# Linear attention: the value and gate projections of a head as one product of 512 columns

## The chip, the cores and the metric

The kernel runs on one core of a Trainium2 chip. The metric is device time in microseconds. Five engines work side by side, each through its own queue in order: TensorE (PE in the rows, its weight loads PEld), VectorE (DVE), ScalarE (ACT), GpSimdE (POOL), and SyncE (SP), which here only issues DMAs. An engine whose next instruction waits does nothing else until that wait is over.

## The reference

Two layers of a hybrid encoder, 512 tokens of width 1024. Each layer normalises, projects, runs three mixers (a state-space mixer, gated linear attention "GLA", and neighbourhood attention), gates and sums them, and ends in an MLP. The change concerns GLA's projections:

```python
h = _rms(x) * norm_mix_w[l]
u = h @ w_in[l]
(z, xbc, dt_f, dt_b, gq, gk, gv, gg, ga_f, ga_b, nq, nk, nv, gate_logits) = jnp.split(u, splits, axis=-1)
...
v = gv.reshape(Bsz, S, GLA_HEADS, GLA_DV)      # 4 heads, 256 value columns each
...
o = gla_chunked(q, k, v, g_f) + _rev(gla_chunked(_rev(q), _rev(k), _rev(v), _rev(g_b)))
o = _rms(o) * gla_norm_w[l] * jax.nn.silu(gg).reshape(Bsz, S, GLA_HEADS, GLA_DV)
```

Of a head, `gv` (values) and `gg` (the output gate, through SiLU) are each 512 tokens by 256 columns.

## The kernel before

Every large product is computed three times over in parts, high weights by high input, high by low, low by high, to keep float32 accuracy on the float32r path. Weights come in **granules** of 128 x 1024 numbers (512 KB) in an order fixed by the list `ks`. `wprep` issues the DMA of a granule into a raw tile `wr` (SP queue), ScalarE copies it to the high part `wh` (L285), VectorE subtracts to get the low part `wl` (L287). `wr`, `wh` and `wl` have three buffers each, used in turn, and `wget` keeps three granules in preparation.

`feat` makes a product with features down the partitions: 8 steps of 3 matmuls of 512 columns (L304 to L306), 24 in all, one granule. `token` makes one with tokens down the partitions, as GLA needs for values and gates: for each of four blocks of 128 tokens, 8 steps of 3 matmuls of 256 columns (L321 to L323). One call serves the values of a head, a second one the gate, with two granules each: 96 matmuls a call, 192 a head, 1536 in the kernel (4 heads, 2 layers). Results land in PSUM tiles `pt` of 128 x 512, two token blocks in one. These and the `pf` tiles of `feat` share a pool `mm` of **two** buffers, used in turn: each new `pt` or `pf` has to wait until the one before the last has been read out. ScalarE reads `pt` out into `G_gvg` (L643), four reads of 128 x 256 a call: plain copies for the values, SiLU for the gate.

`gla_proj(h)` runs the two `token` calls, then `feat` for q and k. `gla_mix(h)` follows: from the small product `G_ga` come, for each of two directions `d`, Abs, Exp and Ln on ScalarE (L670, L673, L674), a subtraction on GpSimdE (L676), a scan on VectorE (L682), and three more Exp on ScalarE (L685, L686, L692). Its matrix part needs q and k. ScalarE has to load a table (ACT_TABLE_LOAD) when it goes from one of SiLU, Exp or Ln to another.

The order of the calls is: projection 0, mix 0, first branch product (16 `feat`), projection 1, mix 1, projection 2, mix 2, projection 3, mix 3. The instructions of each engine are then put into an order by a scheduler ahead of time; `hp()` marks weight preparation and PSUM reads as urgent. Once built, the order on an engine is fixed.

Of the kernel before, what the change touches and what calls it, by code (L numbers as in the profile page):

```python
# [9 lines left out]
F32R = mybir.dt.float32r  # L10
I32 = mybir.dt.int32
AF = mybir.ActivationFunctionType
# [58 lines left out]
def host_arrays(w):  # L71

    w = {k: np.asarray(v) for k, v in w.items()}
    f = np.float32

    def feat(m):
        return m.reshape(KT, P, P).transpose(1, 0, 2).reshape(P, D)

    pk = np.empty((L, NG, P, D), f)
    for l in range(L):  # L80
        wi = w["w_in"][l]
        br = (w["w_branch_na"][l], w["w_branch_gla"][l], w["w_branch_ssd"][l])
        gorder = (2, 1, 0)
        for k, i in KIDX.items():
            o = pk[l, i]
            n = k[0]
            if n in ("nk", "nq", "nv", "gq", "gk", "xs", "B", "C", "z"):
                base = {"nk": O_NK, "nq": O_NQ, "nv": O_NV, "gq": O_GQ, "gk": O_GK, "xs": O_XBC,
                        "B": O_XBC + 1024, "C": O_XBC + 1280, "z": O_Z}[n]
                o[:] = feat(wi[:, base + P * k[1]: base + P * (k[1] + 1)])  # L90
            elif n == "sm":
                ga = wi[:, O_GA: O_GA + 32]
                o[:] = feat(np.concatenate([ga, ga, ga, wi[:, O_DT: O_DT + 32]], axis=1))
            elif n == "gvg":
                h, q = k[1], k[2]
                c = (O_GV, O_GG)[q // 2] + 256 * h
                m = wi[NT * (q % 2): NT * (q % 2 + 1), c: c + 256]
                o[:] = m.reshape(4, P, 256).transpose(1, 0, 2).reshape(P, D)
            elif n == "gate":
                c = O_GATE + D * gorder[k[1]] + P * k[2]  # L100
                o[:] = feat(wi[:, c: c + P])
            elif n == "br":
                o[:] = feat(br[k[1]][:, P * k[2]: P * (k[2] + 1)])
            elif n == "wo":
                o[:] = feat(w["w_out"][l][:, P * k[1]: P * (k[1] + 1)])
            elif n == "f1":
                o[:] = feat(w["w_ff1"][l][:, P * k[1]: P * (k[1] + 1)])
            elif n == "f2":
                q, j = k[1], k[2]
                o[:] = feat(w["w_ff2"][l][D * q: D * (q + 1), P * j: P * (j + 1)])  # L110

    col = np.zeros((L, P, NCOL), f)
    a2 = np.zeros((L, P, 2, NT), f)
    for l in range(L):
        c = col[l]
        c[:, C_NMIX: C_NMIX + 8] = w["norm_mix_w"][l].reshape(8, P).T
        c[:, C_NMLP: C_NMLP + 8] = w["norm_mlp_w"][l].reshape(8, P).T
        c[:, C_CW: C_CW + 60] = w["ssd_conv_w"][l].reshape(5, 12, P).transpose(2, 1, 0).reshape(P, 60)
        c[:, C_CB: C_CB + 12] = w["ssd_conv_b"][l].reshape(12, P).T
        c[:, C_SSDN: C_SSDN + 8] = w["ssd_norm_w"][l].reshape(8, P).T  # L120
        c[:, C_GLAN: C_GLAN + 2] = w["gla_norm_w"][l].reshape(2, P).T
        c[:, C_WQ] = np.concatenate([w["na_q_norm_w"][l]] * 2)
        c[:, C_WK] = np.concatenate([w["na_k_norm_w"][l]] * 2)
        c[:, C_GBF: C_GBF + 4] = w["gla_a2_bias_f"][l].reshape(4, P).T
        c[:, C_GBB: C_GBB + 4] = w["gla_a2_bias_b"][l].reshape(4, P).T
        c[:, C_D: C_D + 8] = np.repeat(w["ssd_d"][l].reshape(8, 2).T, 64, axis=0)
        c[:, C_ALOG: C_ALOG + 32] = np.concatenate([w["ssd_a_log_f"][l], w["ssd_a_log_b"][l]])[None]
        c[:, C_DTB: C_DTB + 32] = np.concatenate([w["ssd_dt_bias_f"][l], w["ssd_dt_bias_b"][l]])[None]
        for r in range(3):
            a2[l, 32 * r: 32 * r + 16, 0] = w["gla_a2_f"][l]  # L130
            a2[l, 32 * r + 16: 32 * r + 32, 1] = w["gla_a2_b"][l]


    con = np.zeros((P, NCON), f)
    con[:, K_ID: K_ID + P] = np.eye(P)
    con[:, K_TF: K_TF + P] = np.triu(np.ones((P, P)))
    con[:, K_TB: K_TB + P] = np.tril(np.ones((P, P)))
    con[:, K_ONE: K_ONE + P] = 1.0
    con[:, K_RST: K_RST + NT] = (np.arange(NT) % 64 != 0)[None]
    for t in range(8):  # L140
        con[:64, K_BS + 32 * t + 2 * t] = 1.0
        con[64:, K_BS + 32 * t + 2 * t + 1] = 1.0
    for r in range(32):
        h = r % 16
        con[r, K_OH + r] = 1.0
        con[32 + r, K_OH + r] = 1.0
        if r < 16:
            con[r, K_E + 64 * h: K_E + 64 * (h + 1)] = 1.0
            con[32 + r, K_E + 64 * h: K_E + 64 * (h + 1)] = 1.0


    bias = np.empty((L, 8, 3, P, 2, 256), f)
    pos = np.arange(NT)
    row, colm = (pos // 8) % 8, (pos // 64) * 8 + pos % 8
    for v, cb in enumerate((0, 1, 3)):
        q = np.arange(P) + P * cb
        k = np.arange(256) + NA_START[cb]
        ro = row[k][None, :] - row[q][:, None] + 7
        d = colm[k][None, :] - colm[q][:, None]
        ws = np.clip(colm[q] - 8, 0, 64 - 16)  # L160
        rel = colm[k][None, :] - ws[:, None]
        ok = (rel >= 0) & (rel < 16)
        co = np.clip(d, -15, 15) + 15
        b = np.where(ok[None, None], w["na_rpb"][:, :, ro, co], f(NEG))
        bias[:, :, v] = b.reshape(L, 8, 2, P, 256).transpose(0, 1, 3, 2, 4)

    xt = np.ascontiguousarray(w["x"].reshape(NT, KT, P).transpose(1, 2, 0))
    return {"xt": xt, "pk": pk, "col": col, "a2": a2, "con": con, "bias": bias}
# [31 lines left out]
def trunk(tc, a, out, layers=L, dbg=None):  # L200
    nc = tc.nc
    V, S, G, T = nc.vector, nc.scalar, nc.gpsimd, nc.tensor
    with ExitStack() as ctx:
# [72 lines left out]

        order, pend = [], []

        def wprep(l, key):
            raw = pw.tile([P, D], F32, tag="wr", bufs=3, name=nm("wr"))  # L280
            nc.sync.dma_start(raw, a["pk"][l, KIDX[key]])
            hi = pw.tile([P, D], F32R, tag="wh", bufs=3, name=nm("wh"))
            lo = pw.tile([P, D], F32R, tag="wl", bufs=3, name=nm("wl"))
            with hp():
                S.activation(hi, raw, AF.Copy)  # L285
            with hp():
                V.tensor_tensor(lo, raw, f(hi), ALU.subtract)  # L287
            pend.append((l, key, hi, lo))

        def wget(l, key):  # L290
            while len(pend) < 3 and order:
                wprep(*order.pop(0))
            l_, k_, hi, lo = pend.pop(0)
            assert (l_, k_) == (l, key), (k_, key)
            return hi, lo
# [10 lines left out]
                T.matmul(ps, lhsT=lo[:, c], rhs=rh[k], start=False, stop=k == KT - 1)  # L306
            return ps

        def token(l, keys, rh, rl):

            w = [wget(l, key) for key in keys]
            ps = []
            for b in range(4):
                if b % 2 == 0:
                    ps.append(psm("pt"))
                o = ps[-1][:, 256 * (b % 2): 256 * (b % 2) + 256]
                s = slice(P * b, P * (b + 1))
                for k in range(KT):
                    hi, lo = w[k // 4]
                    c = slice(256 * (k % 4), 256 * (k % 4) + 256)  # L320
                    T.matmul(o, lhsT=rh[k][:, s], rhs=hi[:, c], start=k == 0, stop=False)  # L321
                    T.matmul(o, lhsT=rh[k][:, s], rhs=lo[:, c], start=False, stop=False)  # L322
                    T.matmul(o, lhsT=rl[k][:, s], rhs=hi[:, c], start=False, stop=k == KT - 1)  # L323
            return ps

        def lnexp(after):

# [54 lines left out]
        for l in range(layers):  # L382
# [225 lines left out]
            def branch(b, j, bh, bl, g_=None):  # L608
# [9 lines left out]
                if b:  # L618
# [2 lines left out]

            px_ = Phase(tc, f"X{l}", {"xs": 4, "bc": 2}, {})
            ph = Phase(tc, f"G{l}", {"A": 1, "kwT": 2, "st0": (3, 256), "st1": (3, 256), "t1": 3, "t2": 3, "w": 2,
                                     "gvg": 8, "bs": 2, "gst": 1, "q": 1, "k": 1, "a2": (2, 256), "kx": (2, 256)},
                       {"ga": 1, "at": 1, "x": 2, "po": 2})
            ps = feat(l, ("sm", 0), xh, xl)
            with hp():
# [5 lines left out]
            glh, gll = [], []  # L633

            def gla_proj(h):
                v_, g_ = [], []
                for n, (r_, fn) in enumerate(((v_, AF.Copy), (g_, AF.Silu))):
                    ps = token(l, [("gvg", h, 2 * n), ("gvg", h, 2 * n + 1)], xh, xl)
                    for i in range(2):
                        t_ = ph.t("gvg", (P, 2, 256))  # L640
                        for b in (0, 1):
                            with hp():
                                S.activation(t_[:, b], ps[i][:, 256 * b: 256 * b + 256], fn,  # L643
                                             scale=rtok[:, 2 * i + b: 2 * i + b + 1])
                        r_.append(t_)
                ps = feat(l, ("gq", h), xh, xl)
                q_ = ph.t("q")
                with hp():
# [437 lines left out]
```

## Time and profile before

| what | value |
|---|---|
| median of 3 runs | 2444.17 us (2443.42 to 2446.34) |
| the profiled execution's own time | 2445.34 us |
| its span in the trace | 2443.6 us |
| TensorE busy | 2428.9 us, 99% of the span |
| ScalarE busy | 1157.9 us, 47% |
| VectorE busy | 1435.6 us, 59% |
| granted TensorE clock | 1.0 |

The time of a run and its span differ by 1.7 us, what lies around the span. Layer 0's GLA runs from about 214 to 545 us, layer 1's from about 1427 to 1760 us; neighbourhood attention goes ahead of it, the state-space mixer follows. In the rows, `x48` is a count, a duration in us stands behind a start, and the bracket says how long the engine had been idle and what it waited for.

### The profile page before, as it was taken

The numbers are of one execution on the slowest core, as the hardware profiler recorded it, in microseconds if no ns is written. First come the engines' busy times: TensorE is split into PE (matmuls) and PEld (weight loads), VectorE is DVE, ScalarE is ACT, GpSimd is POOL, SyncE is SP. The second block draws the span as 40 slices with busy tenths as digits, with TensorE's granted clock in tenths as the row PEclk, the third lists the DMA queues.
The fourth block names the chain that finished last, engine by engine and source line by source line (L and its number), as shares of the span: only waits on it lengthen the run. The fifth ranks groups of instructions, "written<-read, shape, count | busy, mean of one in ns | idle before, by whom it ended". The sixth has DMA issues, their size and how long they took to land.

```text
span 2443.6 us, 32635 instructions
## 1 busy us (share of the span) xinstructions
PE 2428.9 (99%) x12656; PEld 2063.0 (84%) x12656; DVE 1435.6 (59%) x2156; ACT 1157.9 (47%) x2055; POOL 393.3 (16%) x333
## 2 busy tenths in 40 slices
PE   9999999999999999999999999999999999999999
PEld 7899889987888888888888998899888888888887
DVE  6786534587976553443457755345989665534443
ACT  4475425556855342332335754265578543422321
POOL 3132101112431210000122321011134212100000
PEclk9999999999999999999999999999999999999999
DMA  5231222224533323223333222222245332232222
GB/s 183 89 105 63 90 87 79 72 77 134 166 112 126 100 96 97 95 95 100 124 125 97 86 69 88 87 73 85 78 139 168 102 129 95 95 100 98 93 97 87
DMA packets 84603, 249.38 MB, mean 102 GB/s; under 512 B 9824, under 2 KB 15840, under 8 KB 84448
## 3 DMA queue, kind: packets, MB, share of 16 engines
q1 hardware_dynamic: 84016, 246.85, 30.8%
q8 instruction: 100, 1.64, 0.3%
q10 hardware_dynamic: 432, 0.45, 0.1%
q14 instruction: 55, 0.45, 0.1%
HBM read 242.80 MB, written 4.46 MB: 101 GB/s over the span
## 4 chain that ended last, share of the span: by engine, by line
PE 96%; DMA 1%; DVE 1%; ACT 1%; issue 0%; SPq 0%; DVEq 0%
PE pf L305 14%; PE pf L304 14%; PE pf L306 14%; PE F_pf L304 11%; PE F_pf L306 11%; PE F_pf L305 11%; PE pt L322 3%; PE pt L323 3%; PE pt L321 3%; PE N_po L580 2%; PE N_pt L570 1%; PE S_x L956 1%; PE S_py L945 1%; PE N_sc L554 1%; PE N_sc L555 1%; PE G_x L743 1%
## 5 line engine op out<-in xcount | busy, mean ns | idle before, releaser
L285 ACT ACTIVATE wh<-wr 128x1024 fp32r<-128x1024 f32 x378 | 400.3, 1059 | 926.4 <-PE F_pf L305 429.7
L287 DVE TENSOR_TENSOR wl<-wr,wh 128x1024 fp32r<-128x1024 f32 x378 | 486.8, 1288 | 179.0 <-ACT wh L285 177.0
L304 PE MATMUL pf<-xh,wh 128*128 128x512 f32 x1232 | 485.6, 395 | 6.7 <-DVE gl L603 3.8
L305 PE MATMUL pf<-xl,wh 128*128 128x512 f32 x1232 | 486.3, 395 | 0.2 <-DVE xl L349 0.2
L306 PE MATMUL pf<-xh,wl 128*128 128x512 f32 x1232 | 485.1, 394 | 0.0
L304 PEld LDWEIGHTS pf<-xh,wh 128*128 128x128 f32 x1232 | 232.2, 189 | 57.1 <-DVE gl L603 4.6
L306 PEld LDWEIGHTS pf<-xh,wl 128*128 128x128 f32 x1232 | 232.1, 188 | 49.2 <-issue 1.5
L305 PEld LDWEIGHTS pf<-xl,wh 128*128 128x128 f32 x1232 | 232.1, 188 | 47.9 <-DVE xl L349 0.9
L304 PE MATMUL F_pf<-Ah,wh 128*128 128x512 f32 x640 | 248.3, 389 | 0.0
L305 PE MATMUL F_pf<-Al,wh 128*128 128x512 f32 x640 | 247.7, 389 | 0.0
L306 PE MATMUL F_pf<-Ah,wl 128*128 128x512 f32 x640 | 247.7, 389 | 0.0
L306 PE MATMUL F_pf<-xh,wl 128*128 128x512 f32 x512 | 200.0, 391 | 0.0
L305 PE MATMUL F_pf<-xl,wh 128*128 128x512 f32 x512 | 199.2, 389 | 0.0
L304 PE MATMUL F_pf<-xh,wh 128*128 128x512 f32 x512 | 199.2, 389 | 0.0
L1063 DVE TENSOR_TENSOR F_x<-F_x,F_pf 128x512 f32<-128x512 f32 x64 | 44.0, 687 | 206.7 <-PE F_pf L306 206.7
L322 PE MATMUL pt<-wl,xh 128*128 128x256 f32 x512 | 146.2, 286 | 0.0
L321 PE MATMUL pt<-wh,xh 128*128 128x256 f32 x512 | 145.4, 285 | 0.0
L323 PE MATMUL pt<-wh,xl 128*128 128x256 f32 x512 | 144.9, 284 | 0.0
L306 PEld LDWEIGHTS F_pf<-Ah,wl 128*128 128x128 f32 x640 | 120.1, 188 | 25.0
L305 PEld LDWEIGHTS F_pf<-Al,wh 128*128 128x128 f32 x640 | 120.2, 188 | 24.9
L304 PEld LDWEIGHTS F_pf<-Ah,wh 128*128 128x128 f32 x640 | 120.1, 188 | 24.9
L1056 DVE SCALAR_TENSOR_TENSOR F_v<-F_pf,rx 128x512 f32<-128x512 f32 x64 | 44.1, 691 | 159.6 <-PE F_pf L306 159.5
(315 smaller groups left out, 4243.0 us busy)
## 6 DMA issues: line engine op xcount, KB each, us to landing
wr<-pk SPq DMA_DIRECT2D x378, 512.0 KB, 3.3
N_bias<-bias SPq DMA_DIRECT2D x48, 256.0 KB, 2.8
S_E<-acd SPq DMA_DIRECT2D x32, 256.0 KB, 4.4
S_eB<-acd SPq DMA_DIRECT2D x32, 256.0 KB, 3.7
S_eb<-ead SPq DMA_DIRECT2D x64, 96.0 KB, 3.6
F_x<-xt SPq DMA_DIRECT2D x15, 256.0 KB, 5.4
xd<-F_x SPq DMA_DIRECT2D x8, 256.0 KB, 2.0
F_x<-xd SPq DMA_DIRECT2D x8, 256.0 KB, 5.5
```

The source lines that it names most:

```text
L285: S.activation(hi, raw, AF.Copy)
L287: V.tensor_tensor(lo, raw, f(hi), ALU.subtract)
L304: T.matmul(ps, lhsT=hi[:, c], rhs=rh[k], start=k == 0, stop=False)
L305: T.matmul(ps, lhsT=hi[:, c], rhs=rl[k], start=False, stop=False)
L306: T.matmul(ps, lhsT=lo[:, c], rhs=rh[k], start=False, stop=k == KT - 1)
L321: T.matmul(o, lhsT=rh[k][:, s], rhs=hi[:, c], start=k == 0, stop=False)
L322: T.matmul(o, lhsT=rh[k][:, s], rhs=lo[:, c], start=False, stop=False)
L323: T.matmul(o, lhsT=rl[k][:, s], rhs=hi[:, c], start=False, stop=k == KT - 1)
L554: T.matmul(sc[:, i], lhsT=q_[hh][:, qs], rhs=kh[hh][:, kr], start=True, stop=False)
L580: T.matmul(po[:, P * cb: P * (cb + 1)], lhsT=z_[:, c: c + P], rhs=pts[hh][:, i, kb], start=hh + kb == 0, stop=hh + kb == 2)
L1056: V.scalar_tensor_tensor(v_, ps, 0.0, rbc, ALU.max, ALU.mult)
L1063: V.tensor_tensor(xT[j], xT[j], ps, ALU.add)
```

## The change

`token` is called once a head, with four granules. A granule now holds 256 input rows of values and gate side by side, so that a matmul has 512 columns (256 of values, 256 of gate) and a token block fills a whole `pt` tile. That makes 96 matmuls of 512 columns a head in place of 192 of 256. All four granules have to be at hand together; the fourth gets a buffer of its own in the GLA phase (`own`, tiles `G_wh`, `G_wl`), and the next two granules are asked for when the first two have been used for the last time. The order is written out: token blocks 0 and 1 through all granules, then 2 and 3. `done` reads a block out: one copy, one SiLU.

```diff
-        def wprep(l, key):
+        def wprep(l, key, own=None):
             raw = pw.tile([P, D], F32, tag="wr", bufs=3, name=nm("wr"))
             nc.sync.dma_start(raw, a["pk"][l, KIDX[key]])
-            hi = pw.tile([P, D], F32R, tag="wh", bufs=3, name=nm("wh"))
-            lo = pw.tile([P, D], F32R, tag="wl", bufs=3, name=nm("wl"))
+            if own:
+                hi, lo = own.t("wh", (P, D), F32R), own.t("wl", (P, D), F32R)
+            else:
+                hi = pw.tile([P, D], F32R, tag="wh", bufs=3, name=nm("wh"))
+                lo = pw.tile([P, D], F32R, tag="wl", bufs=3, name=nm("wl"))
...
+        def wfill(n=3):
+            while len(pend) < n and order:
+                wprep(*order.pop(0))
...
+            wfill()
+            wprep(*order.pop(0), own)
+            w = []
...
+            ps = {}
+            for n, (g, b) in enumerate(((0, 0), (0, 1), (1, 0), (1, 1), (2, 0), (3, 0), (2, 1), (3, 1),
+                                        (0, 2), (1, 2), (0, 3), (1, 3), (2, 2), (3, 2), (2, 3), (3, 3))):
+                if g == 0:
+                    ps[b] = psm("pt")
                 s = slice(P * b, P * (b + 1))
...
+                hi, lo = w[g]
+                for k in (2 * g, 2 * g + 1):
+                    c = slice(NT * (k % 2), NT * (k % 2 + 1))
+                    T.matmul(ps[b], lhsT=rh[k][:, s], rhs=hi[:, c], start=k == 0, stop=False)
+                    T.matmul(ps[b], lhsT=rh[k][:, s], rhs=lo[:, c], start=False, stop=False)
+                    T.matmul(ps[b], lhsT=rl[k][:, s], rhs=hi[:, c], start=False, stop=k == KT - 1)
+                if g == 3:
+                    done(b, ps[b])
+                if n == 11:
+                    wfill(2)
...
+                def done(b, ps):
+                    for n, (t_, fn) in enumerate(((v_, AF.Copy), (g_, AF.Silu))):
+                        with hp():
+                            S.activation(t_[b // 2][:, b % 2], ps[:, 256 * n: 256 * n + 256], fn,
+                                         scale=rtok[:, b: b + 1])
+
+                token(l, [("gvg", h, i) for i in range(4)], xh, xl, ph, done)
```

The scheduler's order moves with it, on ScalarE above all. The first place is head 1 of layer 0, on ScalarE, from the read-out of token blocks to the weights of q and k. `wh_37..` and `wh_39..` are the high weights that follow the head's own in the kernel before; `G_t` with `G_ga` and `G_bs` is `gla_mix(1)`. Before:

```order
L692 ACTIVATE G_w_3795<-G_w_3795 128x512 [waits Pool_49]
L285 ACTIVATE wh_3591<-wr_3589 128x1024 [waits DMAHW5_49,PE_49]
L643 ACT_TABLE_LOAD
L643 ACTIVATE G_gvg_3696<-pt_3644,tcol_648 128x256 [waits PE_49]
L643 ACTIVATE G_gvg_3696<-pt_3644,tcol_648 128x256
L285 ACTIVATE wh_3701<-wr_3699 128x1024 [waits DMAHW6_49]
L285 ACTIVATE wh_3734<-wr_3732 128x1024 [waits DMAHW7_49,PE_49]
L285 ACTIVATE wh_3923<-wr_3921 128x1024 [waits DMAHW0_49,DVE_49,PE_49]
L670 ACTIVATE G_t_72_3782<-G_ga_3780,col_120 128x512 [waits PE_49]
L673 ACT_TABLE_LOAD
L673 ACTIVATE G_t_72_3782<-G_t_72_3782 128x512 [waits Activation_49]
L674 ACT_TABLE_LOAD
```

The same place of the changed kernel, where L660 is the read-out, L288 the copy of weights, L688 to L710 the mix (`wh_3471` and `wh_3477` are the weights of q and k, `pt_3443` is token block 2):

```order
L691 ACTIVATE G_t_78_3592<-G_t_78_3592 128x512 [waits Activation_49]
L692 ACT_TABLE_LOAD
L692 ACTIVATE G_t_78_3592<-G_t_78_3592 128x512 [waits Activation_49]
L703 ACT_TABLE_LOAD
L703 ACTIVATE G_t_78_3592<-G_bs_3614 128x512 [waits DVE_49]
L704 ACTIVATE G_t_79_3593<-G_bs_3614 128x512
L710 ACTIVATE G_w_3620<-G_w_3620 128x512 [waits Pool_49]
L288 ACTIVATE wh_3471<-wr_3469 128x1024 [waits DMAHW4_49,PE_49]
L288 ACTIVATE wh_3477<-wr_3475 128x1024 [waits DMAHW5_49,PE_49]
L660 ACTIVATE G_gvg_3374<-pt_3443,tcol_648 128x256 [waits PE_49]
L660 ACT_TABLE_LOAD
L660 ACTIVATE G_gvg_3376<-pt_3443,tcol_648 128x256
```

Before, the second direction's chain of the mix stood behind the read-out of the last block and the weights that come next; now that chain stands ahead of the read-out of block 2 and ahead of the weights of q and k.

The second place is TensorE where the head's token product ends and q begins. Before:

```order
L321 MATMUL pt_3644<-wh_3475,xh_182 128x256
L322 MATMUL pt_3644<-wl_3476,xh_182 128x256
L323 MATMUL pt_3644<-wh_3475,xl_183 128x256
L304 MATMUL pf_3705<-xh_154,wh_3585 128x512 [waits Activation_49]
L305 MATMUL pf_3705<-xl_155,wh_3585 128x512
L306 MATMUL pf_3705<-xh_154,wl_3586 128x512 [waits DVE_49]
```

And now:

```order
L335 MATMUL pt_3456<-G_wh_3385,xh_182 128x512
L336 MATMUL pt_3456<-G_wl_3386,xh_182 128x512
L337 MATMUL pt_3456<-G_wh_3385,xl_183 128x512
L310 MATMUL pf_3515<-xh_154,wh_3471 128x512 [waits PE_49,Activation_49]
L311 MATMUL pf_3515<-xl_155,wh_3471 128x512
L312 MATMUL pf_3515<-xh_154,wl_3472 128x512 [waits DVE_49]
```

In both, q's tile takes the PSUM buffer of the tile before the last: before, `pt_3595`, blocks 0 and 1 of the gate, whose last matmul stands 36 places ahead of q's first; now `pt_3443`, block 2, whose last two matmuls stand only 12 places ahead of q's first.

The third place is head 0 on ScalarE. Before:

```order
L285 ACTIVATE wh_2577<-wr_2575 128x1024 [waits DMAHW2_49]
L643 ACT_TABLE_LOAD
L643 ACTIVATE G_gvg_2685<-pt_2587,tcol_648 128x256 [waits PE_49]
L643 ACTIVATE G_gvg_2685<-pt_2587,tcol_648 128x256
L285 ACTIVATE wh_2583<-wr_2581 128x1024 [waits DMAHW4_49,PE_49]
L643 ACTIVATE G_gvg_2688<-pt_2636,tcol_648 128x256 [waits PE_49]
L643 ACTIVATE G_gvg_2688<-pt_2636,tcol_648 128x256
L285 ACTIVATE wh_2693<-wr_2691 128x1024 [waits DMAHW5_49,DVE_49]
```

And now (`pt_2531` is block 2, `wh_2559` and `wh_2565` the weights of q and k):

```order
L688 ACTIVATE G_t_29_2670<-G_ga_2668,col_120 128x512 [waits PE_49]
L346 ACT_TABLE_LOAD
L691 ACTIVATE G_t_29_2670<-G_t_29_2670 128x512 [waits Activation_49]
L692 ACTIVATE G_t_29_2670<-G_t_29_2670 128x512 [waits Activation_49]
L703 ACTIVATE G_t_29_2670<-G_bs_2687 128x512 [waits DVE_49]
L704 ACTIVATE G_t_30_2671<-G_bs_2687 128x512
L288 ACTIVATE wh_2559<-wr_2557 128x1024 [waits DMAHW2_49,PE_49]
L710 ACTIVATE G_w_2693<-G_w_2693 128x512 [waits DMAHW3_49,Pool_49]
L288 ACTIVATE wh_2565<-wr_2563 128x1024 [waits DMAHW4_49,PE_49]
L660 ACTIVATE G_gvg_2462<-pt_2531,tcol_648 128x256 [waits PE_49]
L660 ACT_TABLE_LOAD
L660 ACTIVATE G_gvg_2464<-pt_2531,tcol_648 128x256
```

Before, nothing of the mix stood among the read-outs of head 0; now the first direction's chain stands between the read-outs of block 1 and block 2.

## Rows read from the trace of the kernel before

**Rows 1.** The page: busy time of each engine, share of the span, instructions.
```profile
PE 2428.9 (99%) x12656; PEld 2063.0 (84%) x12656; DVE 1435.6 (59%) x2156; ACT 1157.9 (47%) x2055; POOL 393.3 (16%) x333
```

**Rows 2.** Busy time by stretch, us: PE, PEld, DVE, ACT, POOL, clock, DMA share, GB/s.
```profile
214.00:372.00 158.00, 158.00 (x908) 139.13 (x907) 72.22 (x113) 65.24 (x110) 17.75 (x16) 1.00 0.24 79
372.00:545.00 173.00, 173.00 (x1082) 156.02 (x1082) 108.39 (x179) 98.81 (x153) 25.11 (x19) 1.00 0.23 74
```

**Rows 3.** What TensorE waited for, whole span: us in total, times, longest.
```profile
PE pf L304 <- DVE gl L603: 3.8, 2, 2.1
```

**Rows 4.** Instructions of the tile pt: duration ns min/median/max.
```profile
L321 PE MATMUL pt<-wh,xh x512: 277/283/467, 217.1 to 1687.8; 128*128 128x256 f32 x171
...
L643 ACT ACTIVATE G_gvg<-pt,tcol x64: 456/468/477, 239.9 to 1688.7; 128x256 f32<-128x256 f32 x64
```

**Rows 5.** Timeline of TensorE, head 1: token product, then q and k.
```profile
376.86 0.40 PE L667 MATMUL G_ga<-G_gst,G_a 96*128 96x512 f32 x1
377.10 0.40 PE L321 MATMUL pt<-wh,xh 128*128 128x256 f32 x2
...
387.18 0.40 PE L304 MATMUL pf<-xh,wh 128*128 128x512 f32 x1
...
398.10 0.40 PE L667 MATMUL G_ga<-G_gst,G_a 96*128 96x512 f32 x1
```

**Rows 6.** Timeline of ScalarE, head 1.
```profile
377.31 0.69 ACT L670 ACTIVATE G_t<-G_ga,col 128x512 f32<-128x512 f32 x1
378.01 1.28 ACT L329 ACT_TABLE_LOAD   x1
379.30 0.63 ACT L673 ACTIVATE G_t<-G_t 128x512 f32<-128x512 f32 x1
...
383.18 0.84 ACT L643 ACTIVATE G_gvg<-pt,tcol 128x256 f32<-128x256 f32 x2 [1.28 <-PE pt L323]
...
385.33 0.63 ACT L685 ACTIVATE G_t<-G_bs 128x512 f32<-128x512 f32 x1
385.87 0.62 ACT L686 ACTIVATE G_t<-G_bs 128x512 f32<-128x512 f32 x1
...
386.91 1.05 ACT L285 ACTIVATE wh<-wr 128x1024 fp32r<-128x1024 f32 x1
```

**Rows 7.** Timeline of ScalarE, GpSimdE and VectorE, head 0: from Ln to the next Exp.
```profile
267.92 0.63 ACT L674 ACTIVATE G_t<-G_t 128x512 f32<-128x512 f32 x1
268.68 1.29 POOL L676 TENSOR_TENSOR G_t<-G_t,G_t 128x512 f32<-128x512 f32 x1 [21.82 <-ACT G_t L674]
270.00 1.22 DVE L682 TENSOR_TENSOR_SCAN G_bs<-con,G_t 128x512 f32<-128x512 f32 x1 [2.72 <-POOL G_t L676]
...
271.26 0.63 ACT L685 ACTIVATE G_t<-G_bs 128x512 f32<-128x512 f32 x1 [0.17 <-DVE G_bs L682]
```

**Rows 8.** Timeline of TensorE, start of projection 1: transposes of the branch.
```profile
363.04 1.03 PE L780 MATMUL G_x<-con,G_gvg 128*128 128x128 f32 x8
```

**Rows 9.** Timelines of ScalarE, TensorE, VectorE at the end of neighbourhood attention.
```profile
236.96 1.08 ACT L572 ACTIVATE N_pT<-N_pt 128x512 f32<-128x512 f32 x2 [4.50 <-PE N_pt L570]
...
239.77 1.05 PE L580 MATMUL N_po<-N_pT,N_vb 128*128 128x128 f32 x8
...
239.99 1.23 DVE L287 TENSOR_TENSOR wl<-wr,wh 128x1024 fp32r<-128x1024 f32 x1 [7.76 <-ACT wh L285]
```

**Rows 10.** Timeline of TensorE: the kernel's start, and its longest later idle time.
```profile
8.38 1.22 PE L304 MATMUL pf<-xh,wh 128*128 128x512 f32 x2 [1.77 <-ACT xh L348]
...
10.41 0.63 PE L306 MATMUL pf<-xh,wl 128*128 128x512 f32 x1
...
14.25 0.75 PE L304 MATMUL pf<-xh,wh 128*128 128x512 f32 x2
...
609.69 0.50 PE L304 MATMUL pf<-xh,wh 128*128 128x512 f32 x1 [2.12 <-DVE gl L603]
610.03 0.39 PE L305 MATMUL pf<-xl,wh 128*128 128x512 f32 x1
```

More of the change, by code (lines that the diff above doesn't have):

```diff
@@ L95, in host_arrays @@
                 h, q = k[1], k[2]
-                c = (O_GV, O_GG)[q // 2] + 256 * h
-                m = wi[NT * (q % 2): NT * (q % 2 + 1), c: c + 256]
-                o[:] = m.reshape(4, P, 256).transpose(1, 0, 2).reshape(P, D)
+                r = slice(256 * q, 256 * (q + 1))
+                m = np.concatenate([wi[r, c + 256 * h: c + 256 * (h + 1)] for c in (O_GV, O_GG)], axis=1)
+                o[:] = m.reshape(2, P, NT).transpose(1, 0, 2).reshape(P, D)
             elif n == "gate":
@@ L288, in wprep @@
             pend.append((l, key, hi, lo))
+        def wfill(n=3):
+            while len(pend) < n and order:
+                wprep(*order.pop(0))
         def wget(l, key):
-            while len(pend) < 3 and order:
-                wprep(*order.pop(0))
+            wfill()
             l_, k_, hi, lo = pend.pop(0)
@@ L307, in feat, with token @@
             return ps
[L309 to L316, printed above, removed]
-                s = slice(P * b, P * (b + 1))
[L318 to L324, printed above, removed]
+        def token(l, keys, rh, rl, own, done):
+            wfill()
+            wprep(*order.pop(0), own)
+            w = []
+            for key in keys:
+                l_, k_, hi, lo = pend.pop(0)
+                assert (l_, k_) == (l, key), (k_, key)
+                w.append((hi, lo))
+            ps = {}
[3 more added lines that the diff above has]
+                    ps[b] = psm("pt")
+                s = slice(P * b, P * (b + 1))
+                hi, lo = w[g]
[8 more added lines that the diff above has]
+                    wfill(2)
         def lnexp(after):
@@ L623, in trunk @@
             ph = Phase(tc, f"G{l}", {"A": 1, "kwT": 2, "st0": (3, 256), "st1": (3, 256), "t1": 3, "t2": 3, "w": 2,
-                                     "gvg": 8, "bs": 2, "gst": 1, "q": 1, "k": 1, "a2": (2, 256), "kx": (2, 256)},
+                                     "gvg": 8, "bs": 2, "gst": 1, "q": 1, "k": 1, "a2": (2, 256), "kx": (2, 256),
+                                     "wh": (1, D), "wl": (1, D)},
                        {"ga": 1, "at": 1, "x": 2, "po": 2})
@@ L635, in gla_proj @@
             def gla_proj(h):
[L636 to L645, printed above, removed]
+                v_ = [ph.t("gvg", (P, 2, 256)) for _ in range(2)]
+                g_ = [ph.t("gvg", (P, 2, 256)) for _ in range(2)]
+                def done(b, ps):
[4 more added lines that the diff above has]
+                token(l, [("gvg", h, i) for i in range(4)], xh, xl, ph, done)
                 ps = feat(l, ("gq", h), xh, xl)
```

## Prediction

> **What bounds the kernel now.** I read the page first: TensorE is busy for 2428.9 us, 99% of a span of 2443.6 us [rows 1]. The reader is to see that only two things can move the time: fewer TensorE microseconds, or new idle time on TensorE. Busy time by stretch says the same of the place of the change: in layer 0's GLA TensorE works without a hole, 158.00 of 158 us and 173.00 of 173 us, at a granted clock of 1.00, while ScalarE works for 65 and 99 us and the DMA engines for about a quarter [rows 2]. The waits of TensorE say how good the cover is: the largest entry of the whole span is 3.8 us, in a normalisation outside GLA [rows 3]. So ScalarE and VectorE have slack on average; what matters is whether one of their results is late at a certain matmul. For that I read the timeline of one head, the part of an average that no busy share shows.
>
> The profiled execution took 2445.34 us, 1.2 us above the median of 2444.17. I make the sum against the former and take the 1.2 off at the end.
>
> **What the wider product removes.** There are 512 matmuls on each of the three lines of `token` (4 heads, 2 layers, 64 a line and head), 1536 together, all 128 x 256. Rows 4 show such a group, a median of 283 ns from issue to end; durations overlap, so the price is the pitch. In head 1, 84 matmuls of 256 columns start between 377.10 and 387.18: 0.120 us each. The 48 of 512 columns that follow take from 387.18 to 398.10: 0.2275 us each [rows 5]. A pair of 256 costs 0.240 and its successor 0.2275, so the change saves 12.5 ns on 768 pairs, **9.6 us**. The successor has the same pattern as the 512-column matmuls of `feat` (two of three share their stationary operand), hence the same pitch.
>
> The Trainium skill ("TensorE: Matmul & The Clock Gate", section "Back-to-back issue gap") gives a single matmul N/2.4 + 2.5 ns at the full clock. By that a pair of 256 costs 218.4 ns, one of 512 215.8, and the change saves 768 x 2.5 ns, 1.9 us in place of 9.6. The trace has a fixed part of about 12.5 ns in a stream of this kernel, and I go by the trace.
>
> **What stays.** ScalarE reads out as many pieces as before, 64 in a group of 0.47 us each [rows 4]; granules, bytes, copies and subtractions are the same, and the order has as many table loads (75) as before. The next granules are asked for when granules 0 and 1 are used up; then 24 matmuls of the head remain, 5.5 us by the pitch above. Copy, subtraction and start cost 1.05 [rows 6] and 1.23 us [rows 9], and the raw data come ahead of that at a quarter of the DMA engines' time [rows 2]. I cost it at nothing. Without that cover each head would pay up to those 2.3 us, 18 us in all; nothing in the order asks for it.
>
> **What the order adds, head 1.** This is the main term. A PSUM tile now holds values and gate of one block, and the two buffers go round by block: block 2 gets block 0's, q's tile gets block 2's. q can start only when ScalarE has read out block 2, copy and SiLU. Before, the tile in question had been done 36 matmuls earlier; now its last two stand 12 matmuls ahead of q. And ScalarE has the whole chain of the second direction of mix 1, then the weights of q and k, ahead of that read-out.
>
> I add up both engines from U, the start of the last matmul of block 0. A reader starts 0.45 us after the start of the last matmul (376.86 to 377.31) [rows 5, 6]. ScalarE then has, in its printed order:
> - copy 0.47, table load 1.28, SiLU 0.47 [rows 4, 6]: until U + 2.7. Table load and three Exp of the first direction, 1.28 + 2 x 0.54 + 0.63 [rows 6]: U + 5.6.
> - Block 1: two reads at a pitch of 0.36 (0.84 for two less 0.47) and a table load: U + 7.8.
> - Abs 0.69, table load 1.28, Exp 0.63, table load 1.28 [rows 6]: the Ln starts at U + 11.65.
> - From Ln over GpSimdE (1.29) and VectorE's scan (1.22) to the next Exp it takes 3.34 us, 267.92 to 271.26 [rows 7]: U + 15.0. Three Exp: U + 16.65. Weights of q and k, 1.05 each: U + 18.7.
> - Read-out of block 2, copy, table load, SiLU, 0.36 + 1.28 + 0.47: U + 20.85, and q starts some 0.1 later, U + 20.95.
>
> TensorE in that time has the small gate product (0.24), 12 matmuls of block 1 and 48 of blocks 2 and 3: 60 x 0.2275 + 0.24 + 0.23 = 14.1 us. It wants q at U + 14.1 and gets it at U + 20.95: a stall of **6.9 us**, in each layer. What waits behind it is all of TensorE, q, k, the whole of mix 1; nothing else is at hand for it, since its order is fixed. Before, the same wait ended long ahead, since the mix stood behind the read-outs.
>
> **Head 0.** Three smaller stalls, worked out in the same way.
> - At the end of neighbourhood attention the head's fourth granule is copied behind two copies `N_pT` of 0.36 to 1.08 us [rows 9], and its subtraction (1.23) follows. TensorE has 8 matmuls of about 1 us to cover it [rows 9]. About 1.0 us is left.
> - Block 0's read-out has a table load between copy and SiLU: 0.45 + 0.47 + 1.28 + 0.47 + 0.1 = 2.8 us. TensorE can cover 1.6 (five matmuls, the small product): 1.2 us.
> - Block 2's read-out stands behind the first direction's chain of mix 0 and the weights of q and k. From T, the start of block 0's last matmul: block 0 read 2.7, block 1 (0.84) 3.5, Abs, table load, Exp (0.69 + 1.28 + 0.63) 6.1, Ln to the next Exp (3.34) 9.5, three Exp and two weights (0.54 + 0.63 + 0.63 + 2 x 1.05) 13.4, read-out (0.36 + 1.28 + 0.47) 15.5, less some 0.2 of overlaps: T + 15.3. TensorE starts block 2 at T + 2.9 and wants q 48 matmuls later, T + 13.95: 1.35 us.
>
> Together 3.6 us a layer. Heads 2 and 3, which run interleaved with the mix before, came out with no wait in the same addition. At the start of projection 1 eight transposes of 1.03 us for the branch stand on TensorE [rows 8], and its 16 `feat` ahead of them; they cover the head's first granules.
>
> **The clock.** At the start of the kernel 9 matmuls take from 10.41 to 14.25 us, 0.427 each, against 0.2275 later [rows 5, 10]: that is the lower of the two levels, 1.2 GHz, and idle time stands ahead of it. An idle time of 2.12 us at 609.69 was followed by a pitch of 0.34 and then 0.23, so the clock held [rows 10]. A wait of 6.9 us is three times that one; the trace has no other of its size. The bounds for what it costs in clock are 0 and 2.9 us a stall (the start ran at half rate from 8.38 to 14.25 us [rows 10], and half of these 5.87 is what it lost). It is nearer to the start's than to 2.12 us, so I take **2.0 us** each, 4.0 in all.
>
> The Trainium skill (the same page, section "HAM oscillation — how this bites in real kernels") also says that a stall of several microseconds between matmuls brings TensorE back at the lower clock; that speaks for the upper part of these bounds, and no row here shows such a stall inside the kernel.
>
> **The sum.** −9.6 + 2 x (6.9 + 3.6) + 4.0 = +15.4 us: 2445.34 + 15.4 − 1.2 = **2459.6 us**.
>
> **The rivals.**
> - *ScalarE's chain is not late* (0.19). ScalarE has 40% slack over the stretch [rows 2]; were its chain ahead of my addition by 7 us, because the first direction's Exp are already done when the block 0 read-out comes and the second direction's Abs needs no wait, all stalls would fall under TensorE's work. Then only the saving stays: 2444.2 − 9.6 = 2434.6, faster. It decides at the read-out of block 2 in head 1: the gain outweighs the loss if the stalls add to less than 4.8 us a layer. Against it: the chain has 14 steps in strict order and 4 table loads, with two engines in between, and each duration has its row.
> - *Only half of it* (0.09). The 6.9 us are lost, but to head 0 nothing, or the chain is about 4 us shorter: −9.6 + 7.2 to 9.6 gives 2441.8 to 2444: no change.
> - *The rule's pitch* (0.05). If a 512-column matmul of `token` costs 2.5 ns less than a pair, since each needs its own weight load, the saving is 1.9 us and the sum +23.1: 2467.3. The rows of `feat` speak against it. The page's gap named above is this case; the trace does not agree with it.
> - *The clock holds, or falls fully.* Inside the forecast: 2455.6 without a loss, 2461.4 with 2.9 us a stall.
>
> **How the numbers follow.** The forecast has 0.67. Its own range is 2449 (stalls a third shorter, no loss of clock: −9.6 + 14) to 2466 (stalls a quarter longer). To hold 8 in 10 the range reaches down over the "half" case: 2441 to 2467; outside is mainly the faster rival. A measurement of this kernel can tell about 0.2%, 4.9 us, from no change, so below 2439.3 is faster: 0.19. Between 2439.3 and 2449.1: 0.09. Above, 0.72.
>
> **What would show it.** In the profile after: a wait of TensorE of about 7 us, twice, ahead of q's first matmul in head 1, ended by ScalarE's read-out `G_gvg` (the SiLU), with ScalarE busy or waiting for the scan all that time; waits of 1.2 to 1.4 us twice in head 0, and none of weight in heads 2 and 3. 512-column matmuls of `pt` at a pitch of 0.2275, and so TensorE busy less by 9.6 us but for the clock; a pitch near 0.43 for some microseconds behind each 7 us wait if the clock falls, 0.23 if not. I would be wrong if q's wait is short, which means that ScalarE is through with mix 1 earlier than I add up, or if a wait for weights (`wl`, VectorE) comes in at another place.

## The result and the profile after

The changed kernel takes 2464.88 us (median of 5 runs, 2463.14 to 2465.78), the kernel before 2445.65 us in the same runs: a ratio of 1.0078, with a 95% interval of 1.0065 to 1.0091. That is 19.2 us slower. The forecast was 2459.6 us, +15.4. The two profiled executions differ by 17.7 us in span (2461.3 against 2443.6), and all that follows is told on these spans.

TensorE's busy time hardly moved (2427.5 us against 2428.9): what the wider products save is taken up by matmuls that run more slowly elsewhere, as the granted clock below shows, and the rest of the loss is idle time. Waits of TensorE, changed kernel, whole span (in us: total, times, longest):

```profile
PE pf L310 <- ACT G_gvg L660: 14.3, 4, 6.4
PE pf L310 <- DVE gl L620: 4.4, 2, 2.3
...
PE pt L335 <- ACT G_gvg L660: 1.9, 2, 0.9
...
PE N_po L597 <- ACT N_pT L589: 0.6, 2, 0.3
PE N_pt L587 <- POOL N_s L583: 0.3, 2, 0.2
```

Two names are new: q (`pf`) and the token product (`pt`) wait for the read-out `G_gvg`, which TensorE never waits for in the kernel before. 14.3 us in 4 times, the longest 6.4: two long waits, one a layer, and two short ones of 0.8. The last two lines are the end of neighbourhood attention.

Where they lie shows in busy time by stretch of layer 0, changed kernel (columns as in [rows 2]): head 0 and the branch; head 1's token product with the wait behind it; its q and k; the rest.

```profile
216.80:366.30 149.50, 147.12 (x731) 123.21 (x730) 67.03 (x105) 64.94 (x108) 14.29 (x15) 1.00 0.25 81
366.30:395.40 29.10, 22.82 (x101) 18.33 (x99) 9.98 (x14) 23.42 (x32) 5.78 (x6) 0.95 0.14 43
395.40:408.20 12.80, 12.72 (x48) 10.41 (x49) 5.39 (x6) 3.71 (x6) 0.00 (x0) 0.85 0.52 165
408.20:564.50 156.30, 156.21 (x767) 130.69 (x765) 103.53 (x180) 77.32 (x127) 17.74 (x13) 1.00 0.22 70
```

The same work in the kernel before, by the same view:

```profile
217.13:363.50 146.37, 146.37 (x823) 128.09 (x822) 66.05 (x104) 62.15 (x106) 16.77 (x15) 1.00 0.25 82
363.50:387.10 23.60, 23.60 (x199) 23.56 (x198) 7.72 (x10) 13.76 (x21) 2.33 (x2) 1.00 0.20 67
387.10:398.30 11.20, 11.20 (x51) 9.28 (x51) 4.98 (x6) 5.22 (x7) 0.00 (x0) 1.00 0.44 140
398.30:556.00 157.70, 157.70 (x959) 140.64 (x957) 108.77 (x186) 87.82 (x139) 22.79 (x17) 1.00 0.22 72
```

The differences are +3.1, +5.5, +1.6 and −1.4 us, together +8.8; layer 1 repeats them, +8.6 in all. Only the last stretch, heads 2 and 3, is a gain. In the second TensorE is busy for 22.82 of 29.10 us while ScalarE is busy for 23.42, where it was 13.76; in the third TensorE is busy and yet slow, at a granted clock of 0.85.

TensorE's timeline at the wait (start, duration, the idle time in the bracket):

```profile
377.93 0.40 PE L335 MATMUL pt<-wh,xh 128*128 128x512 f32 x1
...
388.72 0.40 PE L337 MATMUL pt<-G_wh,xl 128*128 128x512 f32 x1
395.48 0.79 PE L310 MATMUL pf<-xh,wh 128*128 128x512 f32 x1 [6.36 <-ACT G_gvg L660]
396.07 0.63 PE L311 MATMUL pf<-xl,wh 128*128 128x512 f32 x1
...
399.06 0.48 PE L312 MATMUL pf<-xh,wl 128*128 128x512 f32 x1
399.37 0.39 PE L310 MATMUL pf<-xh,wh 128*128 128x512 f32 x1
```

q starts 6.76 us after the last matmul of the token product, 6.5 us more than a pitch. Behind it the matmuls start every 0.427 us until 399.06, then every 0.23: the lower level of [rows 10], 1.2 GHz, for 3.6 us.

And ScalarE's timeline over the same time: the copy of block 0, then from the Abs of the second direction to the SiLU of block 2:

```profile
375.10 0.48 ACT L660 ACTIVATE G_gvg<-pt,tcol 128x256 f32<-128x256 f32 x1 [2.22 <-PE pt L337]
...
382.37 0.68 ACT L688 ACTIVATE G_t<-G_ga,col 128x512 f32<-128x512 f32 x1
...
386.31 0.63 ACT L692 ACTIVATE G_t<-G_t 128x512 f32<-128x512 f32 x1
...
389.65 0.63 ACT L703 ACTIVATE G_t<-G_bs 128x512 f32<-128x512 f32 x1 [1.41 <-DVE G_bs L700]
...
391.31 1.99 ACT L288 ACTIVATE wh<-wr 128x1024 fp32r<-128x1024 f32 x2
393.20 0.45 ACT L660 ACTIVATE G_gvg<-pt,tcol 128x256 f32<-128x256 f32 x1
393.66 1.28 ACT L660 ACT_TABLE_LOAD   x1
394.95 0.47 ACT L660 ACTIVATE G_gvg<-pt,tcol 128x256 f32<-128x256 f32 x1
```

The SiLU ends at 395.42, q starts at 395.48. Between Abs and read-out ScalarE idles once, 1.41 us, for the scan; the rest is its own queue, two weight copies among it.

### The profile page after: what moved, and what is told of

Its sections match the earlier page's. It is cut to its first block, busy times and chain, and to the rows that moved or that the text cites. A ratio compares the mean times of both kernels' runs of the same rounds, so it can differ in the third digit from the quotient of the medians.

```text
span 2461.3 us, 31129 instructions
## 1 busy us (share of the span) xinstructions
PE 2427.5 (99%) x11888; PEld 2024.2 (82%) x11888; DVE 1432.4 (58%) x2156; ACT 1159.1 (47%) x2055; POOL 384.5 (16%) x333
## 4 chain that ended last, share of the span: by engine, by line
PE 90%; DVE 3%; ACT 3%; DMA 2%; issue 1%; POOL 0%; SPq 0%; POOLq 0%; DVEq 0%; ACTq 0%
PE pf L310 14%; PE pf L311 14%; PE pf L312 14%; PE F_pf L310 11%; PE F_pf L312 11%; PE F_pf L311 11%; PE N_po L597 2%; PE pt L336 1%; PE pt L335 1%; PE pt L337 1%; PE N_pt L587 1%; DMA S_E<-acd 1%; PE S_x L974 1%; ACT L660 1%; PE G_x L761 1%
## 5 line engine op out<-in xcount | busy, mean ns | idle before, releaser
L288 ACT ACTIVATE wh<-wr 128x1024 fp32r<-128x1024 f32 x370 | 391.6, 1059 | 903.5 <-PE F_pf L311 429.8
L290 DVE TENSOR_TENSOR wl<-wr,wh 128x1024 fp32r<-128x1024 f32 x370 | 476.1, 1287 | 150.6 <-ACT wh L288 148.9
L310 PE MATMUL pf<-xh,wh 128*128 128x512 f32 x1232 | 486.4, 396 | 21.5 <-ACT G_gvg L660 14.3
L312 PEld LDWEIGHTS F_pf<-xh,wl 128*128 128x128 f32 x512 | 96.1, 188 | 20.5 <-issue 0.5
L310 PEld LDWEIGHTS F_pf<-xh,wh 128*128 128x128 f32 x512 | 96.1, 188 | 20.3 <-issue 0.5
L311 PEld LDWEIGHTS F_pf<-xl,wh 128*128 128x128 f32 x512 | 96.1, 188 | 20.0
```

What stands on the lines that cost most here:

```text
L310: T.matmul(ps, lhsT=hi[:, c], rhs=rh[k], start=k == 0, stop=False)
L311: T.matmul(ps, lhsT=hi[:, c], rhs=rl[k], start=False, stop=False)
```

## The experiments

The theory: ScalarE works off the mix's chain and the weights of q and k ahead of block 2's read-out, and TensorE waits for both. The first rival: the two PSUM buffers, which now go round by block, make q wait whatever ScalarE does. The second: the chain, put back, is only late somewhere else.

**e1_mix_behind.** In the kernel's code, `ro[h]` being the last SiLU of the head (an ordering edge between instructions of one engine, no wait):

```diff
-                    ins = S.activation(t1, ps, AF.Abs, bias=bias)
+                    with tc.issue_after(ro[h].ins) if h == 0 or (h == 1 and d == 1) else nullcontext():
+                        ins = S.activation(t1, ps, AF.Abs, bias=bias)
```

> One ordering edge on ScalarE only: in head 0 the Abs of both directions of the mix, in head 1 the Abs of the second direction, stand behind the SiLU of the head's last token block; the granules, matmuls and tiles stay. If the place of the mix's chain on ScalarE is the cause (it delays both the read-out of block 2 and the weights of q and k), the waits ahead of q vanish: 6.5 us and the 1.9 us of lower clock behind it in head 1, 1.0 us in head 0, twice: 2464.9 - 18.8 = 2446. If two PSUM buffers that go round by block are the cause whatever ScalarE's order, q still waits some 3 us for block 2 and the time stays above 2457. If the mix put back becomes late for the products with q and k, there is a new wait ahead of G_at, and the time lies between, near 2452.

Measured: 2446.21 us (median of 11 runs) against 2445.71 before, a ratio of 1.0000, 0.9991 to 1.0009. The whole loss is gone, 18.7 us by ordering edges on ScalarE alone. TensorE's timeline in head 1 of e1:

```profile
366.27 0.47 PE L335 MATMUL pt<-wh,xh 128*128 128x512 f32 x1
...
369.13 0.40 PE L685 MATMUL G_ga<-G_gst,G_a 96*128 96x512 f32 x1
...
377.67 0.39 PE L685 MATMUL G_ga<-G_gst,G_a 96*128 96x512 f32 x1
377.90 0.40 PE L335 MATMUL pt<-wh,xh 128*128 128x512 f32 x1
...
388.70 0.40 PE L337 MATMUL pt<-G_wh,xl 128*128 128x512 f32 x1
388.94 0.39 PE L310 MATMUL pf<-xh,wh 128*128 128x512 f32 x1
```

q follows one pitch behind the token product. The same two PSUM buffers go round in the same way, so the first rival falls. So does the second: no wait ahead of the mix's products appears, and from q to the end of heads 2 and 3 the work takes as long as in the changed kernel without the lower clock. The edges move more than the chain: in e1 ScalarE's order differs in head 0 as well, with 69 table loads in place of 75, and TensorE's order differs in a few places. e4, below, is the narrower edit.

**e2_q_own_bank.** q's tile of head 1 from a pool that is idle there:

```diff
-                ps = feat(l, ("gq", h), xh, xl)
+                ps = feat(l, ("gq", h), xh, xl, ph.p("x") if h == 1 else None)
```

> Only q's PSUM tile of head 1 is taken from the mix's pool x, which is idle there, so that q needs no read-out of block 2; the order on ScalarE stays. If the bank alone holds q up, the whole wait goes: 2464.9 - 2 x (6.5 + 1.9) = 2448. If the weights of q, copied behind the same chain, are next in line, q starts after their copy, 392.4 instead of 395.5 us in the trace, and the subtraction holds the third matmul until about 393.7: a wait of some 4 us stays, and the clock still falls behind it or not: 2459 to 2461.

Measured: 2460.53 us, a ratio of 1.0062 (1.0048 to 1.0076): 4.4 us of the 18.7. TensorE's timeline of e2 at q, now in the tile `G_x`:

```profile
394.25 0.51 PE L310 MATMUL G_x<-xh,wh 128*128 128x512 f32 x1 [3.28 <-ACT wh L288]
...
395.51 0.80 PE L312 MATMUL G_x<-xh,wl 128*128 128x512 f32 x1 [0.52 <-DVE wl L290]
396.11 0.63 PE L310 MATMUL G_x<-xh,wh 128*128 128x512 f32 x1
```

The releaser has changed from `G_gvg` to `wh`: with the bank free, the weights are next in line, 3.28 us late, and their low part another 0.52. The chain stands ahead of both, and to free one resource gives only the distance to the other. The clock falls here too.

**e3_mix_behind_256.** e1 with every product of 512 columns cut in two (`e` runs over the halves 0 and 256; the same for the other two lines):

```diff
-                    T.matmul(ps[b], lhsT=rh[k][:, s], rhs=hi[:, c], start=k == 0, stop=False)
+                    for e in (0, 256):
+                        o, c = ps[b][:, e: e + 256], slice(NT * (k % 2) + e, NT * (k % 2) + e + 256)
+                        T.matmul(o, lhsT=rh[k][:, s], rhs=hi[:, c], start=k == 0 and e == 0, stop=False)
```

> e1_mix_behind with each matmul of 512 columns of the token product cut into two of 256 into the halves of the same tile; order, granules and read-outs as there. Against e1_mix_behind it shows what the width alone is worth. By the pitches of the two traces, 768 x (0.241 - 0.2297) = 8.7 us more; by the prediction's pitches 9.6; by the single-matmul gap that the prediction set beside them 1.9.

Measured: 2457.91 us, a ratio of 1.0049 (1.0037 to 1.0062), 11.7 above e1. Not all of it is the width. The longest waits of TensorE that e3 has and e1 has not, or has shorter (`S_py`: 1.2 us in e1), are in the state-space mixer, whose order came out otherwise:

```profile
PE S_py L966 <- DVE S_E L938: 2.9, 3, 1.3
PE S_x L977 <- ACT S_st L950: 2.7, 2, 1.7
```

The width alone is cleaner in head 1, which has no wait in either. e3 there:

```profile
366.09 0.36 PE L337 MATMUL pt<-wh,xh 128*128 128x256 f32 x1
...
377.63 0.40 PE L687 MATMUL G_ga<-G_gst,G_a 96*128 96x512 f32 x1
377.86 0.28 PE L337 MATMUL pt<-wh,xh 128*128 128x256 f32 x1
...
389.32 0.40 PE L687 MATMUL G_ga<-G_gst,G_a 96*128 96x512 f32 x1
```

192 matmuls of 256 columns take 11.54 + 11.46 = 23.00 us. In e1 the 96 of 512 take 377.67 − 366.27 less the small product between them (0.23), and 388.94 − 377.90, together 22.21. This head gains 0.79 us by the width; if the other seven gain as much, the kernel gains 6.3.

The first matmul of the same head in the kernel before:

```profile
363.83 0.36 PE L321 MATMUL pt<-wh,xh 128*128 128x256 f32 x1
```

Its 192 matmuls end where q begins, at 387.18 [rows 5]: 23.35 us, less 0.24 for the small product among them, 23.11. Against that e1 gains 0.90 us in this head, 7.2 in the kernel by the same estimate. The halves of e3 are thus not quite the matmuls of the kernel before, and the saving lies between 6.3 and 7.2 us.

**e4_head1_only.** e1 with the condition `h == 1 and d == 1` alone.

> As e1_mix_behind, but with the ordering edge of head 1 alone (the Abs of the second direction behind the SiLU of the last token block); head 0 stays as in the changed kernel. If head 1's wait and the clock behind it are the main term, this gives nearly all of what e1 gave: 2464.9 - 2 x (6.5 + 1.9) = 2448.1, and the wait of 0.8 us ahead of q in head 0 stays in the waits. If head 0's edge did more than its own 1 us, the time is above 2450.

Measured: 2448.45 us (median of 11 runs; ratio 1.0009, 1.0000 to 1.0018). Head 1 carries 16.4 of the 18.7 us. The 2.2 us left for head 0's edge are hardly told apart from nothing, since the intervals of e1 and e4 overlap; the trace shows 1.6 of them, head 0's wait ahead of q, which stays in e4. (The wait of `pt`, 1.9 us, stays in e1 and e4 alike.)

```profile
PE pf L310 <- ACT G_gvg L660: 1.6, 2, 0.8
```

In the traces TensorE's matmuls stand in the same order in e4 as in the changed kernel, and ScalarE has 75 table loads in both. So it is the place of the chain on ScalarE that costs the time, not TensorE's order or the number of loads.

**e5_mix_behind_table.** e1, and SiLU's table asked for ahead of head 0's first read-out (`gi` is the copy that makes `G_gst`):

```diff
                 def done(b, ps):
+                    if h == 0 and b == 0:
+                        with tc.issue_after(gi.ins), hp():
+                            S.preload_act_table_set("silu_and_others")
```

> e1_mix_behind, and in head 0 ScalarE loads SiLU's table ahead of block 0's copy, while it waits for TensorE, and not between copy and SiLU. The order on TensorE is that of e1. If the 1.28 us of the table load are what TensorE waits for ahead of block 2 of head 0 (1.1 us, twice), that wait goes: 2446.2 - 2.1 = 2444. If the read-out is late for another reason, nothing changes: 2446.

Measured: 2444.56 us (median of 11 runs) against 2445.92 before; ratio 0.9994, 0.9985 to 1.0003. ScalarE's timeline of e5 has the load first and the four reads of blocks 0 and 1 behind it without a gap:

```profile
240.53 1.28 ACT L660 ACT_TABLE_LOAD   x1
241.82 1.61 ACT L663 ACTIVATE G_gvg<-pt,tcol 128x256 f32<-128x256 f32 x4
```

The wait of `pt` for `G_gvg` (1.9 us) is gone from the waits. Against e1 the medians differ by 1.6 us, but the two intervals overlap; what is shown is that the wait is gone. Against the kernel before it is no difference that can be told.

**e6_own_first.** e5 with `G_wh` and `G_wl` declared first in the phase's list of tiles, which moves them in SBUF; the order on TensorE and ScalarE is that of e5.

> e5_mix_behind_table with the tiles G_wh and G_wl of the fourth granule at another place of SBUF (the front of the GLA phase's region and not its end); the order on TensorE and ScalarE is the same. In the profiles the matmuls that read G_wh or G_wl have a pitch of 233 ns against 229 for those that read wh or wl. If that comes from where these tiles lie, it moves with the place, to 228 or so, and the token product takes about 1 us less; if it comes from their place in the order (steps 6 and 7 of 8 of a block), it stays at 233. Either is too small to be seen in the time, 2444.6.

Measured, in one run: 2449.89 us, against 2444.56 of e5. Matmuls that read `G_wh` or `G_wl`, the tile view of e6 (duration min/median/max), beside those that read `wh`:

```profile
L335 PE MATMUL pt<-wh,xh x192: 387/389/612, 217.1 to 1690.6; 128*128 128x512 f32 x192
...
L335 PE MATMUL pt<-G_wh,xh x64: 389/397/632, 240.9 to 1694.2; 128*128 128x512 f32 x64
```

389 and 397 ns, in the changed kernel 389 and 396: moving the tiles did not shorten the fourth granule's matmuls, so the old place in SBUF is not what makes them longer. What does is left open. The time went elsewhere, to two waits at the end of neighbourhood attention:

```profile
PE pt L335 <- ACT G_wh L288: 2.4, 2, 1.2
...
PE pt L336 <- DVE G_wl L290: 1.1, 2, 0.5
```

At the new place the copy waits 1.74 us for the last products `N_po` of neighbourhood attention. That their tiles had lain there before, so that the place decides when the copy may start, is the likely reading; no run shows it by itself. Behind these waits the granted clock falls, here in layer 0 and in the same way in layer 1 (busy time by stretch, columns as in [rows 2]):

```profile
243.03:246.45 3.42, 3.42 (x10) 2.65 (x9) 0.43 (x1) 1.25 (x4) 0.00 (x0) 0.50 0.58 182
```

3.42 us at 0.50 lose 1.7 us, twice; the waits add up to 3.5. Together this is 6.9 us, a little more than the 6.5 by which the two spans differ (2448.1 against 2441.6).

## Why the prediction was right

**The bound and the sign.** TensorE was the bound, and the outcome was the sum of a small saving and new waits, as forecast. The likeliest case came true, 3.8 us beyond its difference in the medians, 2.3 in the spans.

**Head 1.** The main term was 6.9 us a layer and measured 6.5. The chain of ScalarE can be laid beside the trace. The copy of block 0 starts at 375.10, which puts U at 374.65. The Ln was expected at U + 11.65 = 386.30 and starts at 386.31; the first Exp behind the scan at U + 15.0 = 389.65 and starts there; the weights at 391.30, and start at 391.31; q at 395.60, and starts at 395.48. Adding up the printed order of an engine with durations from rows was good to some 0.1 us over 21 us. What the prediction did not say is that the weights of q were late as well (e2): it named the bank as the reason, and a cure of the bank alone disappointed in e2, with 4.4 us of 18.7. The cause shown is the place of the chain (e1, e4).

**Head 0.** 3.6 us a layer were forecast as 1.0, 1.2 and 1.35. TensorE's timeline of the changed kernel at the fourth granule and around blocks 2 and q:

```profile
239.28 0.71 PE L335 MATMUL pt<-G_wh,xh 128*128 128x512 f32 x2
240.13 0.49 PE L336 MATMUL pt<-G_wl,xh 128*128 128x512 f32 x1
...
242.56 0.40 PE L685 MATMUL G_ga<-G_gst,G_a 96*128 96x512 f32 x1
243.89 0.50 PE L335 MATMUL pt<-wh,xh 128*128 128x512 f32 x1 [0.93 <-ACT G_gvg L660]
...
255.00 0.39 PE L685 MATMUL G_ga<-G_gst,G_a 96*128 96x512 f32 x1
256.23 0.50 PE L310 MATMUL pf<-xh,wh 128*128 128x512 f32 x1 [0.84 <-ACT G_gvg L660]
```

At blocks 2 and q, from start to start and less a pitch of 0.24, these are 1.09 us, whose cause is the table load (e5), and 0.99. (The prediction's want of q at T + 13.95 is T + 13.8 by its own terms, 2.9 and 48 pitches.) The end of neighbourhood attention shows waits of 0.30 and 0.17 (the copies `N_pT` and the products ahead of them). The low part of the fourth granule comes late too: the matmul that reads it starts 0.85 us behind the first of two others, where two pitches are 0.46, so 0.39 are lost; 0.9 together. That is 2.9. The stretch of head 0 and the branch lost more, its +3.1 and the 0.90 that the wider product saved in it: 4.0. What the other 1.1 us are was not followed up.

**The clock.** 4.0 us were taken, between 0 and 5.8. q and k took 12.80 us where 11.2 − 0.23 would do at the higher level (the small product stood among them before): 1.8 us. In layer 1 TensorE was busy at a granted clock of 0.50 for 3.4 us behind the stall, which is 1.7 lost, 3.5 in all. The Trainium skill ("TensorE: Matmul & The Clock Gate", section "HAM oscillation — how this bites in real kernels") has matmuls come back at the lower clock after such a stall; 6.36 us here and 3.28 us in e2 agree.

**The saving: the step that was mis-sized.** "The change saves 12.5 ns on 768 pairs, 9.6 us" is 7.2 by head 1 of e1 and the kernel before, 6.3 by head 1 of e1 and e3. The 512-column price was borrowed from `feat`, 0.2275 us. In `token` it is (388.72 − 377.93) / 47 = 0.2296, and 0.2300 over 48 in e1; a pair of 256 in e3 costs (389.32 − 377.86) / 48 = 0.239. So the step that failed is "hence the same pitch": the same shape in another product is not the same price. The order of steps differs, and the matmuls on the fourth granule last 7 ns longer. What is not explained is why: in e6 another place in SBUF changed nothing.

**The sum.** With the measured terms it is 2 x (6.5 + 2.9) + 3.5 − 7.2 = +15.1 us against 17.7 in the spans. With 4.0 for the whole stretch of head 0 in place of 2.9, layer 1 taken like layer 0, it is +17.3; the rest lies outside GLA. The losses are then 24.5 us where the forecast had 25.0, and the saving is 7.2 where it had 9.6: nearly all of the 2.3 us by which the forecast fell short is the saving. That the losses agree so well is in part luck, since in head 0 the three terms were 0.7 too large together and 1.1 had no term.

The rule of the Trainium skill set beside it ("TensorE: Matmul & The Clock Gate", section "Back-to-back issue gap", by which the saving would be an estimated 1.9 us) does not agree with the trace: 6.3 to 7.2 us is nearer to the pitch by which the prediction went.

**The rivals.** "ScalarE's chain is not late" was wrong, and e1 shows also that its price was: with the chain out of the way the kernel takes 2446.2, not 2434.6, because the saving is smaller than 9.6 and the waits of head 0 at block 0 and ahead of it remain. In e1's profiled execution (2447.53 us) the clock also fell twice outside GLA, 3.4 us each at 0.50, 1.7 lost each; the three of its eleven runs at a granted clock of 1.000 took 2444.3 to 2444.5 us. "Only half of it" did not happen, in either head. Heads 2 and 3 have no wait, as added up: no wait of TensorE between 408 and 564 us is listed.

## What to carry to other kernels

When a product's tiles change how a small ring of PSUM buffers is handed round, write down who reads each buffer out and add up that engine's printed queue, step by step, up to the read; an engine that is half idle can still be 6 us late. A wait has more than one thing ahead of it: before giving it another buffer, ask what is next in line, and prefer to move the work that delays both. The gain of wider matmuls should be priced in the product that is changed, since 12.5 ns a pair became 8 to 9; here it is worth 6 to 7 us, and even with the chain moved (e1) the structure that it needs costs as much.

## What was not expected of the hardware

The length of one idle time did not tell whether the clock falls. At the same place in layer 0 (the read-out `gl` of a gate product), 2.12 us of idle time were followed by a pitch of 0.34 and 0.23 in the kernel before [rows 10] and in the changed one, but in e1 the clock fell behind 2.08 us:

```profile
609.92 0.80 PE L310 MATMUL pf<-xh,wh 128*128 128x512 f32 x1 [2.08 <-DVE gl L620]
610.52 0.63 PE L311 MATMUL pf<-xl,wh 128*128 128x512 f32 x1
```

The pitch there is 0.427, 1.5 us more than in the kernel before until the next product. In e6 the clock fell behind shorter idle times than these, 1.20 and 0.53 us. Nor is it the kernel that decides at such a place: e1's eleven runs have mean granted clocks from 0.997 to 1.000, and their times go roughly with them, 2447.53 us at 0.997 and 2444.28 at 1.000. So up to 3 us of a difference between two profiled executions can be the clock of one of them; what decides it the runs do not show.
